# Feed-forward input products of a two-layer fp32 trunk: two row halves of TensorE, one accumulation bank each

## Chip, core and metric

The kernel runs on one core of a Trainium2 chip. The metric is the device time of one execution in microseconds (us), lower is better. The profile is of one execution on that core; its span runs from the first instruction to the last. All values are float32. The kernel multiplies them on TensorE in the fp32r format, as two parts.

## What is computed

A trunk of two layers over two streams of 256 tokens with 1024 channels: the context (which is computed by the same weights and is dropped at the end) and the latents (the output). Each layer is a half-step feed-forward, a token mixer, and a second half-step feed-forward; each is wrapped in a norm before, a norm behind, a shift, a scale and a gate. The feed-forward, on which the change bears:

```python
def sandwich(x, fn, mod3, g_pre, g_post, weight):
    shift, scale, gate = mod3
    h = rms_norm(x, g_pre) * (1 + scale) + shift
    return x + weight * gate * rms_norm(fn(h), g_post)

def swiglu(h, w_in, w_out):
    g, u = jnp.split(h @ w_in, 2, axis=-1)      # w_in 1024 x 5632
    return (jax.nn.silu(g) * u) @ w_out         # w_out 2816 x 1024
...
for l in range(DEPTH):                          # DEPTH = 2
    xl = sandwich(xl, ffn0, ...); xc = sandwich(xc, ffn0, ...)
    # the mixer: one input projection, recurrences and convolutions by groups of heads, one output projection
    xl = sandwich(xl, ffn1, ...)
    if not last:
        xc = sandwich(xc, ffn1, ...)
```

So there are four feed-forwards. The first three run on both streams (512 tokens), the last on the latents alone (256 tokens).

## The kernel before

**Layout.** Channels lie on the 128 partitions, tokens along the free axis: x, h and the outputs are 8 tiles of 128 channels by 512 tokens, the context's 256 and then the latents' 256. A weight tile of 128 x 128 is loaded into TensorE as the stationary operand and the 512 tokens stream past it.

**Precision by two parts.** Each operand is split in a high part that fp32r holds exactly and the rest (`split`, L169 to L174, ScalarE makes `hi` and VectorE `lo`). A product of two matrices is three passes: hi x hi, hi x lo, lo x hi. h has the parts `hh` and `hl`, weights `hi` and `lo`. A unit of weights is 1024 channels by 128 columns: with 8 tiles of channels and three passes it takes 24 products (`mm3`, L274), all added up in one bank of 512 float32 (`col_mm`, L282). `pbank` (L102) hands out banks of PSUM in turn; there are 6.

**A feed-forward** (`ffn`, L459) has 22 column pairs, a gate and an up unit each, in three parts of 6, 8 and 8 pairs (`PARTS`). For each pair the 44 units' weights come by DMA in `raw` tiles and are split; `col_mm` is called twice (L496); `evac` (L471 to L478) takes Silu of the gate's bank on ScalarE (L472), multiplies by the up bank on VectorE (L473) and splits the result into `ah`, `al`. At the end of each part the output phase (`out_phase`, L312) multiplies the part's 6 or 8 `ah`, `al` tiles by the output weights and adds them into the 8 tiles of `y`: by a ScalarE copy in the first part, by a VectorE addition (L325) in the others. The first 3 pairs of a feed-forward (6 units) go through `front` (L290) instead: their products are put in the order in which the tiles of the next h come.

**The pool `t`.** `tt_()` takes tiles of 128 x 512 float32 from one pool of `NT` = 28 buffers (L30). In a feed-forward it holds 8 tiles of `y`, the parts' `ah` and `al` (up to 16), and the sums of the norms (3). A tile that finds the pool full waits until the oldest tile's last reader is done. The mixers take their arrays from the same pool.

**The handover to the next sub-layer** (`Norms`, L351 to L442). While the last part's output tiles of y come, `add` (L378) makes three squares or products of a tile: two by ScalarE (L384, L386), one by VectorE (L387, `sq`, from a pool of 3 buffers), and adds them into three running sums `acc` (L390; two by GpSimd and one by VectorE, by `JACC`). The first tile's are written into the sums' tiles directly. Behind the last tile of a stream, `scales` (L394) sums over the partitions with products by ones (`st`), GpSimd takes the power -1/2 (`rsqrt`, L241), `update` (L418) broadcasts that over the partitions by TensorE (`rb`, L244 to L248) and begins the residual, and `forward` (L428) broadcasts the next input's scale and makes the tiles of the next h one by one (VectorE L270, L271, L262, L256). The two streams' last six output tiles are kept apart, so that the first stream's chain runs while TensorE does the second stream's products.

**What sets the order.** TensorE's instructions run in the order in which the code issues them. `Products` (L106) keeps a clock of the products issued (columns over 2400, in us), and `after` puts the steps of the norms (`LAG`, `STEP`) behind so much of later products. A wait in an instruction holds all that stands behind it on its engine. VectorE, ScalarE and GpSimd run their own queues in an order that the tile framework fixes when the program is built, from the order of the code and from when buffers come free.

Of the kernel before, what the change touches and what calls it, by code (L numbers as in the profile page):

```python
# [8 lines left out]
F32 = mybir.dt.float32  # L9
# [5 lines left out]
P = 128  # L15
# [14 lines left out]
NT, NRAW, NSPL = 28, 4, 6  # L30
SKEW = 6
# how much of the products (Products.clock) goes between the tiles of the next input, for the first stream and the second
STEP = (1.8, 0.4)
# places in h for tiles of the output
# [5 lines left out]
# how much of the products goes ahead of the sums over channels, of the first and of the second scales, likewise  # L40
# [3 lines left out]
# the last mixer's output tiles in banks  # L44
OUT_AT = ((0, 0), (0, 1), (1, 0), (1, 1), (2, 0), (3, 0), (4, 0), (5, 0))
# the last mixer's last tiles of the output, for all of its tiles in turn and then tile by tile
LATE = ((0,), (1, 2, 3))
MANUAL = {mybir.EngineType.PE}
# the parts of the mixers in the order in which they are issued: projections (small) and recurrences (capital)
# [3 lines left out]
# the last feed-forward's last units whose output products are put in the order of its tiles  # L53
TAIL = 4
# the last feed-forward's units behind which the residual is turned
TURN = 5
# tiles of modulation vectors made beside each feed-forward's units: in the first part, in the others, in the output phase
PUMP = {(0, 0): (2, 2, 2), (0, 1): (0, 2, 1), (1, 0): (0, 2, 1)}
# the start's steps, in the order in which they are issued: pairs of tiles of x (loads x, squares a), the tokens' scales (t, y),
# the conditioning vectors (c, rows d, e), units (loads u, parts w), the first modulation vectors for a pair of tiles by the  # L60
# tensor engine (loads q, products r, s, end f), their scale or shift for a tile by VectorE (loads v, b, sums V, B), pairs of
# tiles of h (h), the products that can be issued of the tiles before a given one (*), the mixer's small arrays (z) and decays (l)
# [5 lines left out]
# columns of the packed vectors, in units of [128, 1]  # L68
# [13 lines left out]
def backbone(ctx: ExitStack, tc: tile.TileContext, xT, vecs, crow, w_mod, w_in, w_out, w_mi, w_mo, w_lru, w_cm, b_cm, lam, w_last, out):  # L82
# [23 lines left out]
    class Products:  # L106
        """The tensor engine's queue, kept in the order of issue; what waits for other engines is put behind later products."""
# [4 lines left out]
        def matmul(self, dst, lhsT, rhs, start, stop):  # L112
            te.matmul(dst, lhsT=lhsT, rhs=rhs, start=start, stop=stop)  # L113
            self.clock += max(rhs.free_size(), 64) * (4 if rhs.dtype == F32 else 1) / 2400
            while not self.inside and self.later and self.later[0][0] <= self.clock:
                self.next()
# [59 lines left out]
    def load_split(src, shape, park=None):  # L176
        """A unit's two parts; park takes them to a place in h, idle at a phase's end: 0, 1 in the latents' half, 2, 3 in the other."""
        raw = wp.tile(shape, F32, tag="raw", name=nm("raw"), bufs=NRAW)
        nc.sync.dma_start(raw, src)
        if park is None:  # L180
            hi = wp.tile(shape, F32R, tag="hi", name=nm("hi"), bufs=NSPL)
            lo = wp.tile(shape, F32R, tag="lo", name=nm("lo"), bufs=NSPL)
        else:
            o = (P * park + SEQ) % T
            hi, lo = (t[:, :shape[1], o:o + P] for t in (hh, hl))
        h = shape[1] // 2
        for a, b in ((0, h), (h, shape[1])):
            split(raw[:, a:b], hi[:, a:b], lo[:, a:b])
        return hi, lo

# [53 lines left out]
    def broadcast(r):  # L244
        """[P tokens, 2] to [P, 256 tokens], on all partitions"""
        rb = ps_st.tile([P, SEQ], F32, tag="st", name=nm("rb"))
        for tt in range(2):
            te.transpose(rb[:, tt * P:(tt + 1) * P], r[:, tt:tt + 1].to_broadcast([P, P]), ident)  # L248
        return rb
# [24 lines left out]
    def mm3(dst, wh, wl, mh, ml, ks):  # L274
        """Three passes for two parts of each operand; the last of ks, which may come late, at the end."""
        ops = [(wh(k), x(k)) for k in ks[:-1] for x in (mh, ml)] + [(wl(k), mh(k)) for k in ks[:-1]]
        k = ks[-1]
        ops += [(wh(k), mh(k)), (wh(k), ml(k)), (wl(k), mh(k))]
        for i, (w, x_) in enumerate(ops):
            pe.matmul(dst, lhsT=w, rhs=x_, start=(i == 0), stop=(i == len(ops) - 1))  # L280

    def col_mm(w, a, b):  # L282
        """A loaded unit of 128 columns against the tokens a : b of h."""
        hi, lo = w
        p = pbank()
        mm3(p[:, :b - a], lambda k: hi[:, k, :], lambda k: lo[:, k, :],
            lambda k: hh[:, k, a:b], lambda k: hl[:, k, a:b], range(KT))
        return p

    def front(ws, plan, done):  # L290
        """The first units, channel by channel as h comes: plan has token ranges with units, done takes their products."""
        for a, b, us in plan:
# [9 lines left out]
            for k in range(KT):  # L302
                for i, (u, p) in enumerate(zip(us, aps)):
                    hi, lo = ws[u]
                    # one group a bank: its first product clears the bank
                    first, last = i % per == 0, i % per == per - 1 or i == len(us) - 1
                    for j, (w, h) in enumerate(((hi, hh), (hi, hl), (lo, hh))):
                        pe.matmul(p, lhsT=w[:, k, :], rhs=h[:, k, a:b],
                                  start=(first and k == 0 and j == 0), stop=(last and k == KT - 1 and j == 2))
            done(us, aps, a, b)  # L310

    def out_phase(ms, load, ah, al, y, nk, ranges_of, on_y, part, nparts, npump=0):  # L312
        """y[m] (+)= the product with the unit's weights, over token ranges; on_y(m, a, b) at the end."""
# [31 lines left out]
    # mean squares of the streams' tokens, with EPS  # L345
    msq = {}

    class Norms:
        """A sub-layer's output norm, residual and the next input norm, fed with the output tile by tile. With x' = x + r G y
        the mean square of x' is that of x, 2 r mean(x G y) and r^2 mean((G y)^2), so that both norms' scales come from sums  # L350
        over the tiles of y."""  # L351

        def __init__(self, segs, y, l, i, nxt, turn=False):
            self.segs, self.y, self.l, self.i, self.nxt = segs, y, l, i, nxt
            self.ready = False
            # whether a stream is the first or the second to come
# [87 lines left out]
    # the streams whose next input is on its way  # L444
# [4 lines left out]
    def unit_pieces(source):  # L449
        """Units for the next sub-layer, by halves."""  # L450
# [8 lines left out]
    def ffn(l, f, segs, nxt, plan, skew_out, turn=False):  # L459
# [5 lines left out]
        for part in range(NPART):  # L465
# [29 lines left out]
            for j in range(j0, nj):  # L495
                evac(j, *[col_mm(w, lo_t, hi_t) for w in load_in(j)], lo_t, hi_t)  # L496
# [12 lines left out]
    def ffn_last(l, f, plan):  # L509
        """The last feed-forward, on the latents, its output with the tokens on the partitions and gathered over all of the units  # L510
        in place, so that the output norm's scales need no way across the partitions."""
# [3 lines left out]
        # the residual, with the tokens on the partitions  # L515
# [64 lines left out]
        for tt in range(2):  # L580
            yg = [tt_() for _ in range(2)]
            for h in range(2):
                for j in range(max(NJ - TAIL, 0), NJ):
                    out_mm(j, tt, h)
                # 1 / 32 is the root of 1 / D
# [14 lines left out]
    def gain_row(l, v, s, h):  # L600
        """Half of a modulation vector as rows on all partitions."""
# [15 lines left out]
    def mixer(l, segs, nxt, plan, skew_out, order_of, next_unit=None):  # L617
        """segs: the streams whose output is wanted; both run the recurrence."""
# [24 lines left out]
        # the units of the input projection, then of the output projection, loaded two ahead of their use  # L643
# [66 lines left out]
        def lru_decay(c):  # L710
            for c, d, b in heads[2 * c:2 * c + 2]:
                e, r = tt_(), rs[c, d]
                # u = tanh(w / 2), e = exp(-w), w = 8 r softplus(-lambda); m = 1 - exp(-w) = u (1 + e)
# [3 lines left out]
                # (m - 2) m = -(1 - a^2)  # L717
# [87 lines left out]
        # the output projection of one stream: all tiles at once, the recurrent heads' part last, in float32's own  # L805
        # four passes
# [44 lines left out]
        # one stream: with x' = x + r G y the mean square of x' is that of x, 2 r mean(x G y) and r^2 mean((G y)^2),  # L851
        # so both norms' scales come from sums over the tiles of y
# [111 lines left out]
    def quarter_rows(q, k0):  # L964
        """Both vectors for two tiles by products with rows of weights, the inputs' chunks in turn on quarters of the columns."""
# [40 lines left out]
    def decays():  # L1006
        # softplus(-lambda) = max(-lambda, 0) + log1p(exp(-|lambda|)), log1p by its atanh series
# [157 lines left out]
def _layout(i):  # L1165
# [15 lines left out]
    # [l, vector, tile, output channel, inputs]; of the first two vectors some pairs of tiles by inputs: for each  # L1181
    # chunk of inputs [inputs, vector, tile, output channel], two such blocks a tile
# [14 lines left out]
    # [l, pair of heads, input, (direction, gate), output], block diagonal over the pair  # L1197
# [27 lines left out]
```

## Time and profile before

| | |
|---|---|
| median of 2 runs | 1649.24 us (1648.44 to 1650.04) |
| profiled execution, its span | 1648.9 us |
| TensorE busy | 1615.8 us, 98% |
| VectorE busy | 1165.1 us, 71% |
| ScalarE busy | 735.3 us, 45% |
| GpSimd busy | 121.2 us, 7% |
| read from memory | 247.39 MB, 151 GB/s over the span |

The profiled execution's own time is its span; what lies around it is within the 1.6 us by which the runs differ. Engines are PE (TensorE's products), PEld (TensorE's loads of weights, which can lie under products), DVE (VectorE), ACT (ScalarE), POOL (GpSimd) and SP (SyncE, which issues the DMAs). A busy PE is one with a product under way, which is more than the time that its stream of columns takes: products overlap, and the pitch from one start to the next is what they cost. An idle stretch of an engine is printed before the instruction that ended it, with what that instruction waited for. PEclk is the granted clock of TensorE as a share of full speed.

### The profile page before, as it was taken

Reading aid. Unit: us, or ns where it says so; the run is one execution under the profiler, and the core shown is the slowest. Engines: PE = TensorE matmul, PEld = TensorE weight load, DVE = VectorE, ACT = ScalarE, POOL = GpSimd, SP = SyncE. Lnnn points to the kernel's source line nnn. Section 1 sums busy time; section 2 is a strip of 40 time slices with the busy share of each in tenths; the row PEclk is TensorE's granted clock in tenths of the full one; section 3 lists DMA queues with packets and bytes.
Section 4 is the critical chain, followed back from the end, with each engine's and each line's share of the span. In section 5 each row is a group of like instructions: output and inputs, shape, how many; then the busy total and the mean of one; then the engine's idle time right before and its main releaser. Section 6 shows DMA issues by size and latency. Waiting matters only on the chain.

```text
span 1648.9 us, 23405 instructions
## 1 busy us (share of the span) xinstructions
PE 1615.8 (98%) x8832; PEld 1374.5 (83%) x8832; DVE 1165.1 (71%) x2183; ACT 735.3 (45%) x1377; POOL 121.2 (7%) x166
## 2 busy tenths in 40 slices
PE   6999999999999999999999999999999999999998
PEld 3788888889977998888888998888888998789997
DVE  4899898458689777867753887767433788875554
ACT  5524222244597662332233463322132469764543
POOL 0000000005000510000000410000000420000000
PEclk9999999999999999999999999999999999989999
DMA  9577666430323225655552215655422216245552
GB/s 369 187 226 264 201 228 219 146 127 28 103 71 110 86 88 191 209 168 175 182 163 80 99 46 198 219 167 176 140 90 90 103 52 202 80 138 195 179 192 77
DMA packets 73906, 249.97 MB, mean 152 GB/s; under 512 B 8384, under 2 KB 10048, under 8 KB 73792
## 3 DMA queue, kind: packets, MB, share of 16 engines
q1 hardware_dynamic: 73216, 247.94, 44.7%
q8 instruction: 69, 1.13, 0.3%
q10 hardware_dynamic: 576, 0.52, 0.1%
q14 instruction: 45, 0.37, 0.1%
HBM read 247.39 MB, written 1.05 MB: 151 GB/s over the span
## 4 chain that ended last, share of the span: by engine, by line
PE 90%; DVE 6%; ACT 2%; issue 1%; POOL 1%; DMA 0%; SPq 0%; POOLq 0%; DVEq 0%; ACTq 0%
PE mm L113 88%; PE st L113 1%; DVE x L271 1%; DVE sq L387 1%; DVE z L270 1%; DVE tmp L262 0%; DVE t L390 0%; DVE hl L256 0%; PE mod L113 0%; POOL rs L241 0%; DMA x<-in_xT 0%; ACT hh L263 0%; DVE ms L410 0%; DVE t L325 0%; POOL t L390 0%
## 5 line engine op out<-in xcount | busy, mean ns | idle before, releaser
L173 ACT CAST hi<-raw 128x512 fp32r<-128x512 f32 (+1 forms) x596 | 343.0, 610 | 675.0 <-PE mm L113 488.0
L113 PE MATMUL mm<-hh,hi 128*128 128x512 f32 (+1 forms) x1840 | 627.6, 350 | 1.1 <-ACT hh L263 1.1
L113 PE MATMUL mm<-hl,hi 128*128 128x512 f32 (+1 forms) x1840 | 626.0, 348 | 1.3 <-DVE hl L256 0.5
L174 DVE TENSOR_TENSOR lo<-raw,hi 128x512 fp32r<-128x512 f32 (+1 forms) x596 | 388.9, 683 | 158.3 <-ACT hi L173 155.2
L113 PE MATMUL mm<-hh,lo 128*128 128x512 f32 (+1 forms) x1840 | 469.3, 347 | 0.0
L113 PEld LDWEIGHTS mm<-hh,hi 128*128 128x128 f32 x1840 | 348.1, 190 | 52.5 <-ACT hh L1075 2.5
L113 PEld LDWEIGHTS mm<-hl,hi 128*128 128x128 f32 x1840 | 349.3, 190 | 50.9 <-DVE hl L1081 1.4
L113 PEld LDWEIGHTS mm<-hh,lo 128*128 128x128 f32 x1840 | 328.1, 190 | 47.2
L196 DVE SCALAR_TENSOR_TENSOR junk<-raw,cb 128x1024 bf16<-128x1024 f32 x256 | 312.8, 1222 | 69.0 <-DMA raw<-in_w_mod 65.4
L113 PE MATMUL mm<-t,hi 128*128 128x512 f32 (+1 forms) x1056 | 240.6, 367 | 0.0
L113 PEld LDWEIGHTS mm<-t,hi 128*128 128x128 f32 x1056 | 182.8, 188 | 35.7 <-issue 0.2
L390 POOL TENSOR_TENSOR t<-t,sq 128x256 f32<-128x256 f32 x112 | 95.0, 863 | 716.9 <-ACT sq L384 705.5
L113 PE MATMUL mm<-t,lo 128*128 128x512 f32 (+1 forms) x528 | 131.5, 367 | 0.0
L113 PEld LDWEIGHTS mm<-t,lo 128*128 128x128 f32 x528 | 92.6, 188 | 17.7
L473 DVE TENSOR_TENSOR sg<-sg,mm 128x512 f32<-128x512 f32 (+1 forms) x72 | 46.0, 639 | 82.9 <-PE mm L113 81.5
L113 PE MATMUL mm<-t,hh 128*128 128x256 f32 x512 | 72.1, 282 | 0.0
L113 PEld LDWEIGHTS mm<-t,hh 128*128 128x128 f32 x512 | 66.1, 188 | 0.5
L173 ACT CAST t<-sg 128x512 fp32r<-128x512 f32 (+1 forms) x94 | 50.7, 541 | 30.6 <-DVE sg L473 27.5
L263 ACT ACTIVATE hh<-tmp,modv 128x256 fp32r<-128x256 f32 x72 | 42.5, 597 | 34.6 <-DVE tmp L262 34.3
L325 DVE TENSOR_TENSOR t<-t,mm 128x256 f32<-128x256 f32 (+1 forms) x66 | 35.3, 536 | 29.2 <-PE mm L113 29.0
L174 DVE TENSOR_TENSOR t<-sg,t 128x512 fp32r<-128x512 f32 (+1 forms) x94 | 55.1, 587 | 1.0 <-ACT t L173 1.0
L113 PE MATMUL mm<-hi,t 128*128 128x512 f32 x176 | 55.1, 394 | 0.0
(177 smaller groups left out, 1199.3 us busy)
## 6 DMA issues: line engine op xcount, KB each, us to landing
raw<-in_w_in SPq DMA_DIRECT2D x176, 512.0 KB, 3.6
raw<-in_w_mod SPq DMA_DIRECT2D x128, 512.0 KB, 4.2
raw<-in_w_out SPq DMA_DIRECT2D x48, 512.0 KB, 3.3
raw<-in_w_mi SPq DMA_DIRECT2D x36, 512.0 KB, 4.2
raw<-in_w_last SPq DMA_DIRECT2D x22, 512.0 KB, 3.2
raw<-in_w_out SPq DMA_DIRECT2D x24, 384.0 KB, 3.6
t<-in_w_mod SPq DMA_DIRECT2D x32, 256.0 KB, 5.8
raw<-in_w_mo SPq DMA_DIRECT2D x8, 512.0 KB, 4.0
```

The lines of the kernel that those rows point to most:

```text
L113: te.matmul(dst, lhsT=lhsT, rhs=rhs, start=start, stop=stop)
L173: sc.copy(hi, src)
L174: ve.tensor_tensor(lo, src, hi.bitcast(F32), op=OP.subtract)
L196: ve.scalar_tensor_tensor(junk, raw.rearrange("p k c -> p (k c)"), 1.0, cb[:, s], op0=OP.mult, op1=OP.mult, accum_out=modv[l][:, v, m, s:s ...
L263: sc.activation(hh[:, m, a:b], tmp, AF.Identity, scale=A, bias=B)
L270: ve.tensor_tensor(z, y[m][:, a:b], rb, op=OP.mult)
L271: ve.scalar_tensor_tensor(x[:, m, a:b], z, mcol(l, 3 * i + 2, m, s), x[:, m, a:b], op0=OP.mult, op1=OP.add)
L325: ve.tensor_tensor(y[m][:, a:b], y[m][:, a:b], p[:, :b - a], op=OP.add)
L387: ve.scalar_tensor_tensor(q[2], y, G, x[:, m, a:b], op0=OP.mult, op1=OP.mult)
L390: (gp if JACC[c] == "g" else ve).tensor_tensor(acc[c], acc[c], q[c], op=OP.add)
L473: ve.tensor_tensor(sg[:, :b - a], sg[:, :b - a], pu[:, :b - a], op=OP.mult)
```

## The change

The units of the first three feed-forwards behind the staged first ones (`ffn`, L496 of before) go through a new function, `col_mm2`, with two banks. Each product on 128 rows (channels) becomes two, one on the rows 0 to 63 and one on the rows 64 to 127, with the same 512 columns; the first half's products are summed in one bank, the second half's in the other. The two follow one another, half by half, through all 24. Then ScalarE copies the first bank to a tile `half` in SBUF (from 2 buffers), VectorE adds the second bank to it, and `evac` reads those tiles where it read banks. The pool `t` has 26 buffers in place of 28. The clock of `Products` counts a product of 64 rows as half, so that the norms' steps fall behind as many units as before. `front`, the output phases, the mixers and the last feed-forward stay as they are. The remaining lines of the diff take comments away.

```diff
-NT, NRAW, NSPL = 28, 4, 6
+NT, NRAW, NSPL = 26, 4, 6
...
         def matmul(self, dst, lhsT, rhs, start, stop):
             te.matmul(dst, lhsT=lhsT, rhs=rhs, start=start, stop=stop)
-            self.clock += max(rhs.free_size(), 64) * (4 if rhs.dtype == F32 else 1) / 2400
+            self.clock += max(rhs.free_size(), 64) * (4 if rhs.dtype == F32 else 1) / 2400 * (0.5 if lhsT.shape[0] == 64 and lhsT.dtype == F32R else 1)
...
+    def col_mm2(w, a, b):
+
+        hi, lo = w
+        ps2 = [pbank(), pbank()]
+        for i, (t, h) in enumerate([e for k in range(KT) for e in ((hi[:, k], hh[:, k]), (hi[:, k], hl[:, k]))]
+                                   + [(lo[:, k], hh[:, k]) for k in range(KT)]):
+            for r, p in enumerate(ps2):
+                rows = slice(64 * r, 64 * r + 64)
+                pe.matmul(p[:, :b - a], lhsT=t[rows], rhs=h[rows, a:b], start=i == 0, stop=i == 3 * KT - 1)
+        t = hp.tile([P, T], F32, tag="half", name=nm("half"), bufs=2)
+        sc.copy(t[:, :b - a], ps2[0][:, :b - a])
+        ve.tensor_tensor(t[:, :b - a], t[:, :b - a], ps2[1][:, :b - a], op=OP.add)
+        return t
...
-                evac(j, *[col_mm(w, lo_t, hi_t) for w in load_in(j)], lo_t, hi_t)
+                evac(j, *[col_mm2(w, lo_t, hi_t) for w in load_in(j)], lo_t, hi_t)
```

How the order moves is shown at two places, with the names of the program and its numbers of buffers.

TensorE at the first changed unit of the first feed-forward, before (`mm` is a bank, `hh` and `hl` the parts of h, `hi` the weights):

```order
L113 MATMUL mm_458<-hh,lo_427 128x512
L113 MATMUL mm_626<-hh,hi_612 128x512
L113 MATMUL mm_626<-hl,hi_612 128x512
L113 MATMUL mm_626<-hh,hi_612 128x512
L113 MATMUL mm_626<-hl,hi_612 128x512
```

The same place after the change:

```order
L113 MATMUL mm_458<-hh,lo_427 128x512
L113 MATMUL mm_626<-hh,hi_612 128x512
L113 MATMUL mm_627<-hh,hi_612 128x512
L113 MATMUL mm_626<-hl,hi_612 128x512
L113 MATMUL mm_627<-hl,hi_612 128x512
```

Each product has become two, into the banks 626 and 627, in turn.

TensorE at the end of the first feed-forward, before (`st` are the products with ones of the first stream, from the three sums `t_2771` to `t_2773`; `mm_3082` is the bank of an output tile of the second stream):

```order
L113 MATMUL mm_3082<-t_2660,hl 128x256
L113 MATMUL mm_3082<-t_2733,hh 128x256
L113 MATMUL st_3105<-ones,t_2771 128x2 x2
L113 MATMUL st_3105<-ones,t_2772 128x2 x2
L113 MATMUL st_3105<-ones,t_2773 128x2 x2
L113 MATMUL mm_3082<-t_2734,hh 128x256
L113 MATMUL mm_3082<-t_2733,hl 128x256
L113 MATMUL mm_3138<-t_2170,hh 128x256
L113 MATMUL mm_3138<-t_2171,hh 128x256
```

The same step after the change (the sums are `t_3835` to `t_3837`, `mm_4394` is the bank of the second stream's last output tile, `rb` are the broadcasts, `hi_4451` and on the next sub-layer's weights):

```order
L113 MATMUL mm_4394<-t_3797,hh 128x256
L113 MATMUL mm_4394<-t_3798,hh 128x256
L113 MATMUL mm_4394<-t_3797,hl 128x256
L113 MATMUL st_4169<-ones,t_3835 128x2 x2
L113 MATMUL st_4169<-ones,t_3836 128x2 x2
L113 MATMUL st_4169<-ones,t_3837 128x2 x2
L248 MATMUL rb_4216<-ident,rs_4178 128x128 x2
L248 MATMUL rb_4251<-ident,rs_4188 128x128 x2
L113 MATMUL mm_4547<-hh,hi_4451 128x256
L113 MATMUL mm_4548<-hh,hi_4467 128x256
L113 MATMUL mm_4679<-hh,hi_4483 128x256
```

The products with ones and both broadcasts have moved from between the output tiles to behind the last of them, with the next input's products right after.

VectorE at the same place, before (`t_108` and `t_109` are tiles of y; L325 adds a bank to one; L387 writes a product for the third sum, `t_2773` itself for the first tile of each stream; `lo` are weights):

```order
L325 TENSOR_TENSOR t_108<-t_108,mm_2745 128x512
L174 TENSOR_TENSOR lo_3388<-raw_3385,hi_3387 128x512
L387 SCALAR_TENSOR_TENSOR t_2773<-t_108,modv_106,x 128x256 x2
L174 TENSOR_TENSOR lo_3388<-raw_3385,hi_3387 128x512
L174 TENSOR_TENSOR lo_3396<-raw_3393,hi_3395 128x512 x2
L174 TENSOR_TENSOR lo_3404<-raw_3401,hi_3403 128x512 x2
L325 TENSOR_TENSOR t_109<-t_109,mm_2788 128x512
```

And after the change, where L339 is the line of the bank's addition, L401 that of the product and L404 that of the sums:

```order
L339 TENSOR_TENSOR t_113<-t_113,mm_4300 128x256
L174 TENSOR_TENSOR lo_4492<-raw_4489,hi_4491 128x512 x2
L339 TENSOR_TENSOR t_114<-t_114,mm_4343 128x256
L401 SCALAR_TENSOR_TENSOR t_3837<-t_108,modv_106,x 128x256 x2
L401 SCALAR_TENSOR_TENSOR sq_3971<-t_111,modv_106,x 128x256
L404 TENSOR_TENSOR t_3836<-t_3836,sq_3970 128x256
L401 SCALAR_TENSOR_TENSOR sq_4014<-t_112,modv_106,x 128x256
L339 TENSOR_TENSOR t_115<-t_115,mm_4394 128x256
```

The third sum's first write stood behind the addition to the first tile of y (`t_108`); it now stands behind the addition to the last-but-one tile (`t_114`), just ahead of the last (`t_115`).

## Rows read from the trace of the kernel before

**Rows 1.** The page, part 1: busy us (share of the span) xinstructions.

```profile
PE 1615.8 (98%) x8832; PEld 1374.5 (83%) x8832; DVE 1165.1 (71%) x2183; ACT 735.3 (45%) x1377; POOL 121.2 (7%) x166
```

**Rows 2.** Timeline 133.5 to 134.2, PE and PEld: start us, us, engine line op.

```profile
133.55 0.40 PE L113 MATMUL mm<-hh,hi 128*128 128x512 f32 x1
133.56 0.19 PEld L113 LDWEIGHTS mm<-hl,hi 128*128 128x128 f32 x1
...
133.78 0.40 PE L113 MATMUL mm<-hl,hi 128*128 128x512 f32 x1
```

**Rows 3.** Windows: us, then PE, PEld, DVE, ACT, POOL, PEclk, DMA, GB/s.

```profile
82.00:164.00 82.00, 82.00 (x353) 66.06 (x353) 78.96 (x141) 26.53 (x50) 0.00 (x0) 1.00 0.74 243
164.00:247.00 83.00, 83.00 (x358) 66.86 (x357) 73.89 (x128) 24.04 (x43) 0.00 (x0) 1.00 0.65 214
```

**Rows 4.** The chain that ended last, 386 to 425: start us, us, what.

```profile
388.40 1.25 PE st L113 x12
...
413.12 6.30 PE mm L113 x29
...
419.64 3.42 PE mm L113 x29
```

**Rows 5.** Timeline of the same handover, PE, the broadcasts.

```profile
391.34 0.38 PE L248 MATMUL rb<-ident,rs 128*128 128x128 f32 x2
...
393.89 0.43 PE L248 MATMUL rb<-ident,rs 128*128 128x128 f32 x2 [0.41 <-POOL rs L241]
```

**Rows 6.** Groups by form, PE: busy us, mean ns | idle before.

```profile
L113 PE MATMUL mm<-hh,hi 128*128 128x512 f32 x1040 | 413.2, 397 | 0.0
...
L113 PE MATMUL mm<-t,wbd 128*128 128x512 f32 x64 | 28.5, 594 | 0.0
...
L113 PE MATMUL mod<-t,cs 128*32 128x512 f32 x64 | 9.7, 677 | 0.0
```

**Rows 7.** Timeline 34 to 37, PE: products on quarters of the columns.

```profile
34.03 1.92 PE L113 MATMUL mod<-t,cs 128*32 128x512 f32 x16
```

**Rows 8.** Groups by form, the other engines: busy us, mean ns | idle before.

```profile
L390 POOL TENSOR_TENSOR t<-t,sq 128x256 f32<-128x256 f32 x112 | 95.0, 863 | 716.9 <-ACT sq L384 705.5 <-DVE sq L387 9.4 <-DVE msq L413 2.0
...
L473 DVE TENSOR_TENSOR sg<-sg,mm 128x512 f32<-128x512 f32 x60 | 41.1, 684 | 81.6 <-PE mm L113 81.5
...
L387 DVE SCALAR_TENSOR_TENSOR sq<-t,modv,x 128x256 f32<-128x256 f32 x56 | 36.2, 646 | 4.1 <-ACT t L323 1.2 <-ACT sq L384 0.5
...
L271 DVE SCALAR_TENSOR_TENSOR x<-z,modv,x 128x256 f32<-128x256 f32 x64 | 33.8, 538 | 0.1
...
L256 DVE TENSOR_TENSOR hl<-tmp,hh 128x256 fp32r<-128x256 f32 x72 | 30.9, 433 | 6.8 <-ACT tmp L264 6.3
...
L262 DVE TENSOR_TENSOR tmp<-x,rb 128x256 f32<-128x256 f32 x72 | 29.3, 411 | 6.9 <-PE rb L248 6.8
...
L270 DVE TENSOR_TENSOR z<-t,rb 128x256 f32<-128x256 f32 x64 | 25.7, 411 | 4.5 <-PE rb L248 4.3
...
L323 ACT COPY t<-mm 128x512 f32<-128x512 f32 x26 | 15.1, 581 | 8.1 <-PE mm L113 8.1
```

**Rows 9.** Timeline 1445.5 to 1452, PE: the last mixer's handover.

```profile
1445.53 0.63 PE L605 MATMUL mm<-ident,modv 128*128 128x128 f32 x4
...
1449.21 0.69 PE L248 MATMUL rb<-ident,rs 128*128 128x128 f32 x2 [1.30 <-POOL rs L241]
1451.05 1.22 PE L113 MATMUL mm<-hh,hi 128*128 128x256 f32 x4 [1.15 <-ACT hh L263]
```

**Rows 10.** Windows, PE alone: us, PE busy (x), PEclk, DMA share, GB/s.

```profile
410.00:412.00 2.00, 1.27 (x11) 1.00 0.00 0
414.00:416.00 2.00, 2.00 (x11) 0.50 0.91 307
```

## The prediction

> **What bounds the kernel now.** I read the shares of the engines first. TensorE is busy for 98% of the span, VectorE for 71%, ScalarE for 45% [rows 1]. So a change is worth what it does to the stream of products, or what it puts into that stream as a wait. Second, what one product costs. In the units that the change rewrites a product of 512 columns starts 0.23 us after the one before it (133.55, 133.78) [rows 2], and the windows give the mean: 353 products in 82 us without a gap, 233 ns each [rows 3]. Each load of 128 x 128 weights lasts 0.19 us and begins within 0.01 us of the start of the product before the one that needs it, so it lies under that product [rows 2]. Third, where the slack is: VectorE has 3 us left of 82 in the first window and 9 of 83 in the second [rows 3]. Fourth, the handovers between sub-layers, where the output's last tiles, three running sums over the tiles, two scales and the next input follow one another. At 388.40 the 12 products with ones that finish a stream's sums take 1.25 us in the chain that ended last [rows 4], and the broadcasts follow at 391.34 and 393.89, among products [rows 5]. That overlap is what keeps TensorE at 98%.
>
> **The products.** 114 units change (three feed-forward layers of 44, less 6 each that stay in the first, staged part), each with 24 products: 2736 of the 3120 with 512 columns against h, whose first group of three has the row shown (x1040) [rows 6]. Each becomes two of 64 rows, so 2736 products and 2736 loads are added. The trace has no product of 64 rows. Its nearest rows are the products on quarters of the columns: 16 of them, whose mean duration is 677 ns, take 1.92 us together [rows 6, 7], and the 64 of that group are busy for 9.7 us, where 64 of the same kind on the whole array (the rows of t and wbd) are busy for 28.5 us [rows 6]. Parts of the array therefore run side by side at the price of one. From below, a pair costs the pure stream of 512 columns at 2.4 GHz, the level granted here [rows 3]: 213 ns, 20 less than now. From above, two in turn cost 466 ns. I take 234 to 235, nearest to the quarters: both halves stream the same 512 columns, and the two loads of a pair fit under it, since products of two columns, which only load, start every 104 ns (1.25 us for 12 [rows 4]), 208 for two. That is 2736 x 1.5 ns = **+4 us**, with ends of -55 and +637 us.
>
> The Trainium skill speaks for more (TensorE: Matmul & The Clock Gate, Part 3): weight loads overlap products in flight only where the row groups differ. By that rule loads would stand bare before the change and the halves would hide them. The trace disagrees: loads on all 128 rows lie under products on all 128 rows [rows 2], so I take no gain from it.
>
> **Taking the banks.** Each unit adds a copy of a bank by ScalarE, 581 ns like the copy of the output tiles, and an addition by VectorE, 684 ns like the product after Silu [rows 8]: 66 and 78 us over 114 units. ScalarE has the room. VectorE has not, in the first layer's windows: some 11 units end in the first, 7.5 us more against 3 us left, and 14 in the second, 9.6 us against 9 [rows 3]. A bank pair is wanted again two units later (6 banks, 2 a unit): 2 x 24 x 233 ns = 11.2 us of cover. The lag of some 5 us stays under it, but the addition stands behind weight halves and modulation sums in VectorE's queue. I take **+4 us**, between 0 and 15.
>
> **The smaller pool.** This is the largest term, and it is not in the products. NT falls from 28 to 26. At the end of a feed-forward 27 tiles of that pool are wanted: 8 of y, 16 of ah and al, 3 sums. With 26 the third sum gets its place only when al[0] is read for the last time, by the second of the 24 products of the last output tile. The order shows it: VectorE now writes the third sum after its addition of the last-but-one tile, and the products with ones stand behind the last output product with both broadcasts right behind them and the next input's products after those. Before, some 140 products of the second stream lay over this chain. All of it is now bare, at the ends of the first, second and third feed-forward. With E as the end of the last output product:
> - The third sum starts at E - 2.6 (22 products at 118 ns: 29 took 3.42 us [rows 4]). Two writes by VectorE, 0.65 us each [rows 8]; the first lets GpSimd begin at about E - 2.0.
> - GpSimd then has 13 additions before the first stream's sums are whole: 7 of the third sum, 5 of the first sum, held up because the 3 buffers for squares filled behind the third, and one of the second stream. At 95.0 us for 112 [rows 8], 0.85 each, that is 11.0 us: E + 9.0.
> - From the end of the sums to the first product of the next input the last mixer shows the bare chain: the products before it start at 1445.53 and last 0.63, the second broadcast waits 1.30 for GpSimd, the first product starts at 1451.05 [rows 9], about 5 us. Here half a microsecond of products with ones comes before, and two more GpSimd additions and about four VectorE operations (0.5 us each) of the second stream stand in it: 8 us. E + 17.
> - After an idle stretch the granted clock falls: TensorE is busy for 1.27 of the 2 us from 410, so idle for 0.73, the clock is 0.50 (the 1.2 GHz level) from 414 to 416, and 29 products take 6.30 us where the next 29 take 3.42 [rows 4, 10]. **+3 us**.
> - The second stream's sums lie behind the first's norm on VectorE (8 tiles of 0.41 + 0.54 + 0.41 + 0.43 = 1.79 us [rows 8] plus 5 us of sums, against 17 us of products): **+2 us**.
>
> That is 17 + 3 + 2 = 22 us, three times: **+66 us**, with ends of 10 and 32 each. At the end of the first mixer the sums run along as before, but the products with ones now stand inside the last tile of the second stream, with both broadcasts at its end: of the chain of 5 us some 1 us is covered, plus clock 3 and pace 3: **+10 us** (4 to 20). Inside the mixers the two missing tiles can make parts wait; the order of weights loaded differs there in one place only, so **+1 us** (0 to 10).
>
> Sum: 4 + 4 + 66 + 10 + 1 = +85 us on the profiled 1648.9, which is 0.3 below the median of the runs: **1734 us**.
>
> **The rivals.**
> - Halves in turn. Against it: the quarters of the columns [rows 6, 7]. For it: no row shows halves of the rows. 2736 x 233 = +637, plus 81 for the rest: 2367 us.
> - Halves side by side, but their loads bare, so that a pair costs 233 + 104 = 337 ns: +285 + 81, 2015 us. For it: the load path would be used for 208 of 233 ns, nearly without slack. Against it: loads under products on the same rows [rows 2]. The Trainium skill's page on TensorE (Part 3, measured speedup) gives 3.07-fold for four row tiles, so 1.30 of one product; an estimate from that page puts a pair between 1 and 1.30 of one, up to 303 ns, +192 us; no run here shows it.
> - Not slower: the pair runs at the bare stream of 213 ns because the 20 ns between products hide behind the other half. 2736 x -20 = -55, and the pool's +81 remains: 1675 us, within 2%. It decides from about 215 ns a pair. For it: 233 is 20 above 213. Against it: products of 256 columns start every 118 ns [rows 4], 11 above their 107, so the surplus goes with the columns, which halving the rows leaves as they are.
> - The pool does not bind as I say, because the sums are done soon after their place comes free: 5 us a handover in place of 22, 1649 + 4 + 4 + 25 = about 1682 us. Against it: GpSimd's 13 additions, which the order has behind the third sum.
>
> **How the numbers follow.** My forecast 0.74; halves in turn 0.08; loads bare or partly so 0.08; bare stream 0.06; pool not binding 0.04. About 2% is what a measurement here tells from no change, 33 us. The third and fourth of these lie at that edge, so within 2% gets 0.10, faster 0.02 (a pair would have to cost under 191 ns, below the stream itself), slower 0.88. The range reaches from 1685 (handovers at 12 us, or a pair at 217) to 1840 (handovers at 32, a pair at 260); the two dear cases above it hold most of the rest.
>
> **What would show it.** Right: in the second feed-forward windows of after a pair starts every 230 to 240 ns, the clock stays at 1.00, and TensorE's idle time, 33 us now, is over 80, nearly all in four handovers, before products with ones (released by GpSimd's additions) and before the next input's first products. The clock dips after each. Wrong: starts of a pair 213 or over 300 ns apart; no wait by products with ones for GpSimd; waits inside the units for VectorE's additions of over 15 us in all.

## The result, and the profile after

The changed kernel takes 1919.35 us (median of 2 runs, 1918.46 to 1920.23) against 1649.24 before: a ratio of 1.1639 (95% interval 1.1617 to 1.1661), 270 us slower. The forecast was 1734, range 1685 to 1840. The direction was right, the size was not.

The first part of the page of after, beside [rows 1]:

```profile
PE 1689.6 (88%) x11568; PEld 1416.5 (74%) x11568; DVE 1241.4 (65%) x2297; ACT 801.1 (42%) x1491; POOL 121.9 (6%) x166
```

TensorE has its 2736 products more (11568 in place of 8832) but is busy for only 74 us longer: the products as such did not double in price. It is idle for 227 us (1916.6 less 1689.6), where it was idle for 33. Where, the waits of PE say (engine line waited for: us in total, times, longest us):

```profile
PE mm L113 <- ACT t L173: 97.1, 12, 19.3
PE mm L113 <- DVE half L301: 50.6, 22, 6.7
PE st L113 <- POOL t L404: 27.3, 4, 9.0
PE st L113 <- DVE t L1057: 13.7, 1, 13.7
PE rb L248 <- POOL rs L241: 12.9, 10, 1.6
PE mm L113 <- ACT hh L263: 8.3, 5, 1.8
```

The third, fifth and sixth row are the handovers that the prediction spoke of; the fourth was there before (14.4 us). The first two make 148 us. The first, output products that wait for `ah`, the prediction did not have. The second, units that wait for a bank addition (`half`), is 50.6 us where it named over 15 as a sign of being wrong. The windows of [rows 3] show the same stretches of after (us, then PE, PEld, DVE, ACT, POOL, PEclk, DMA, GB/s):

```profile
82.00:164.00 82.00, 53.24 (x281) 41.08 (x278) 59.81 (x105) 18.29 (x38) 0.00 (x0) 0.81 0.55 170
164.00:247.00 83.00, 76.61 (x612) 60.09 (x610) 58.30 (x99) 25.33 (x48) 0.00 (x0) 1.00 0.50 159
```

TensorE loses 29 of the first 82 us. VectorE, which was expected to be full there, is busy for 60: it is late without being full. The timeline of PE has the longest of these waits, at the first output phase (start us, us, line, op):

```profile
120.29 0.40 PE L113 MATMUL mm<-t,hi 128*128 128x512 f32 x1
139.97 1.65 PE L113 MATMUL mm<-t,hi 128*128 128x512 f32 x3 [19.29 <-ACT t L173]
```

And the chain that ended last shows what held ScalarE's `t` (start us, us, what):

```profile
124.07 3.56 DMA raw<-in_w_mod
...
127.72 1.25 DVE junk L196 x2
...
131.53 1.24 DVE junk L196 x2
...
132.79 3.55 DMA raw<-in_w_mod
...
137.60 0.60 DVE half L301
...
138.66 0.61 DVE sg L487
...
139.30 0.63 ACT t L173
...
139.97 1.22 PE mm L113 x2
```

`junk` is VectorE's sum for a modulation vector (L196 in `mod_tile`): two for each 128 x 1024 tile, each after a DMA into the ring of 4 `raw` buffers that the weights share. The sums belong to the gate at this feed-forward's end and to later sub-layers; nothing at this place needs them. But they stand ahead of the addition in VectorE's queue, each tile's DMA starts when an earlier tile's sums have freed a buffer, and the addition, the multiplication (`sg`), ScalarE's `t` and TensorE wait behind the row of them.

The order of VectorE shows how they came there. Counted in it: the modulation sums that stand ahead of the multiplication of the fourth, fifth and sixth pair of the first feed-forward.

| | 4th | 5th | 6th |
|---|---|---|---|
| before | 6 | 13 | 20 |
| after | 13 | 24 | 33 |

Thirteen more sums at 1.22 us with their DMAs have to be done before the sixth pair's `ah`, for which the output products wait. At the other parts' ends the shift is smaller: 8 sums in the second part of the first feed-forward, 3 or 4 in the first two parts of the next two, none in the third parts. A few are enough. At the end of the second feed-forward's first part it is 4, and TensorE waits for 13.9 us at 786.26, since the DMAs stand one behind another there too (the chain that ended last):

```profile
768.69 3.82 DMA raw<-in_w_mod
...
776.63 4.19 DMA raw<-in_w_mod
```

What the prediction feared most did not come. The timeline of PE and PEld in after, a stretch without waits (a row x2 is one pair, which the units' order puts side by side):

```profile
80.53 0.40 PE L113 MATMUL mm<-hh,hi 64*128 64x512 f32 x2
80.54 0.19 PEld L113 LDWEIGHTS mm<-hl,hi 64*128 64x128 f32 x2
80.77 0.40 PE L113 MATMUL mm<-hl,hi 64*128 64x512 f32 x2
```

A pair starts every 0.23 us, as a product did [rows 2], and both loads begin within 0.01 us of it. The gain is zero and so is the price: at the full clock pairs in after and products before both start every 233.3 ns in the mean.

### The profile page after: what moved, and what is told of

Read it like the earlier page. It is cut to its first block, busy times and chain, and to the rows that moved or that the text cites. A ratio compares the mean times of both kernels' runs of the same rounds, so it can differ in the third digit from the quotient of the medians.

```text
span 1916.6 us, 29041 instructions
## 1 busy us (share of the span) xinstructions
PE 1689.6 (88%) x11568; PEld 1416.5 (74%) x11568; DVE 1241.4 (65%) x2297; ACT 801.1 (42%) x1491; POOL 121.9 (6%) x166
## 4 chain that ended last, share of the span: by engine, by line
PE 55%; DVE 17%; DMA 17%; issue 5%; ACT 3%; POOL 2%; DVEq 0%; SPq 0%; POOLq 0%; ACTq 0%
PE mm L113 53%; DMA raw<-in_w_mod 16%; DVE junk L196 8%; DVE lo L174 3%; DVE half L301 2%; POOL t L404 1%; ACT hi L173 1%; PE st L113 1%; ACT sg L486 1%; PE mod L113 1%; DVE hl L174 1%; DMA raw<-in_w_in 0%; DVE sg L487 0%; DVE sq L401 0%; DVE t L174 0%
## 5 line engine op out<-in xcount | busy, mean ns | idle before, releaser
L113 PE MATMUL mm<-hh,hi 64*128 64x512 f32 (+2 forms) x2752 | 696.9, 375 | 59.1 <-DVE half L301 50.6
L113 PE MATMUL mm<-hl,hi 64*128 64x512 f32 (+2 forms) x2752 | 694.4, 372 | 1.6 <-DVE hl L256 1.0
L113 PEld LDWEIGHTS mm<-hh,hi 64*128 64x128 f32 (+1 forms) x2752 | 449.7, 194 | 126.6 <-DVE half L301 61.7
L113 PEld LDWEIGHTS mm<-hl,hi 64*128 64x128 f32 (+1 forms) x2752 | 452.3, 193 | 51.4 <-DVE hl L256 3.4
L113 PE MATMUL mm<-hh,lo 64*128 64x512 f32 (+2 forms) x2752 | 464.8, 362 | 0.0
L196 DVE SCALAR_TENSOR_TENSOR junk<-raw,cb 128x1024 bf16<-128x1024 f32 x256 | 313.3, 1224 | 228.8 <-DMA raw<-in_w_mod 224.8
L113 PEld LDWEIGHTS mm<-hh,lo 64*128 64x128 f32 (+1 forms) x2752 | 343.0, 188 | 45.6
L113 PE MATMUL mm<-t,hi 128*128 128x512 f32 (+1 forms) x1056 | 257.8, 383 | 102.2 <-ACT t L173 97.1
L404 POOL TENSOR_TENSOR t<-t,sq 128x256 f32<-128x256 f32 x112 | 94.5, 864 | 1374.2 <-ACT sq L398 1316.2
L486 ACT ACTIVATE sg<-half 128x512 f32<-128x512 f32 x57 | 36.1, 633 | 196.2 <-DVE half L301 196.2
L339 DVE TENSOR_TENSOR t<-t,mm 128x256 f32<-128x256 f32 (+1 forms) x66 | 35.6, 540 | 82.8 <-PE mm L113 82.7
L301 DVE TENSOR_TENSOR half<-half,mm 128x512 f32<-128x512 f32 x114 | 77.6, 681 | 11.3 <-ACT half L300 11.3
L300 ACT COPY half<-mm 128x512 f32<-128x512 f32 x114 | 66.2, 581 | 29.0 <-PE mm L113 29.0
```

The costliest lines, as they stand in the source:

```text
L196: ve.scalar_tensor_tensor(junk, raw.rearrange("p k c -> p (k c)"), 1.0, cb[:, s], op0=OP.mult, op1=OP.mult, accum_out=modv[l][:, v, m, s:s ...
L300: sc.copy(t[:, :b - a], ps2[0][:, :b - a])
L301: ve.tensor_tensor(t[:, :b - a], t[:, :b - a], ps2[1][:, :b - a], op=OP.add)
L339: ve.tensor_tensor(y[m][:, a:b], y[m][:, a:b], p[:, :b - a], op=OP.add)
L404: (gp if JACC[c] == "g" else ve).tensor_tensor(acc[c], acc[c], q[c], op=OP.add)
L486: sc.activation(sg[:, :b - a], pg[:, :b - a], AF.Silu)
```

## Experiments

All times are medians (e7 and e8: of one run each, so without an interval) beside runs of the kernel before on the same chip, which gave 1648.7 to 1651.0. Theory A is that the order of VectorE's and ScalarE's queues costs what is not the small pool; its rivals are the additions and the pairs themselves.

**e1, the small pool alone.**

```diff
 (before)
-NT, NRAW, NSPL = 28, 4, 6
+NT, NRAW, NSPL = 26, 4, 6
```

> The kernel before with the pool of 26 buffers and nothing else. Its order has the products with ones and both broadcasts of the first stream behind the last output product at the ends of the first three feed-forwards, as after the change. Theory (the pool is worth what the prediction said, 22 us a handover): 1649 + 66 + 10 + 1 = about 1726 us. Rival (the chain is shorter, as the waits by products with ones in the changed kernel, 27.3 us over 4, and the broadcasts' 12.9 suggest: some 12 to 15 us a handover with the clock): 1685 to 1700 us.

Measured: 1707.65 us, ratio 1.0356 (1.0340 to 1.0371), +59. Between the two expectations. The timeline of PE at the first handover:

```profile
402.14 0.28 PE L113 MATMUL mm<-t,hl 128*128 128x256 f32 x1
411.35 2.72 PE L113 MATMUL st<-ones,t 128*128 128x2 f32 x12 [8.93 <-POOL t L390]
415.35 0.69 PE L248 MATMUL rb<-ident,rs 128*128 128x128 f32 x2 [1.28 <-POOL rs L241]
417.65 0.69 PE L248 MATMUL rb<-ident,rs 128*128 128x128 f32 x2 [1.61 <-POOL rs L241]
420.14 1.01 PE L113 MATMUL mm<-hh,hi 128*128 128x256 f32 x3 [1.81 <-ACT hh L263]
```

From the end of the last output product (402.42) it is 8.93 us to the end of GpSimd's sums, and 17.7 to the next input's first product: the 9.0 and 17 of the prediction. (Its terms behind the sums, 5, 0.5, 1.7 and 2 us, make 9 and not the 8 that it took; 8.8 were measured.) The net is smaller. By the starts of equal-numbered products in the two traces the three handovers cost 14, 16 and 17 us, not 22 each, the first mixer's end 8 in place of 10, and the second mixer's, which the prediction did not count, 3. About 2 of the 17 us are products with ones and broadcasts that TensorE had to run before as well (1.25, 0.38 and 0.43 us) [rows 4, 5]. The low clock was there before at the first handover [rows 10] and, for 3.4 us from 958.5, at the second, so its 3 us were in part counted twice; at the third (1334 to 1338) the clock before was 1.00. No run shows the 2 us for the second stream.

**e2, no copy and no addition** (the sums over the channels 64 to 127 of each tile are left out).

```diff
 (col_mm2 of after)
-        t = hp.tile([P, T], F32, tag="half", name=nm("half"), bufs=2)
-        sc.copy(t[:, :b - a], ps2[0][:, :b - a])
-        ve.tensor_tensor(t[:, :b - a], t[:, :b - a], ps2[1][:, :b - a], op=OP.add)
-        return t
+        return ps2[0]
```

> The changed kernel without the copy and the addition: the second bank is left out of the result, so the sums over half of the channels are missing. Theory A (the order: on VectorE's queue more of the modulation sums stand ahead of each pair's multiplication than before, 13, 24 and 33 in the first part in place of 6, 13 and 20, and TensorE comes to the output phase before VectorE has made ah): the stalls stay, 1850 to 1920 us. Theory B (the additions themselves hold the banks and VectorE): only the small pool is left, 1690 to 1735 us.

Measured: 1927.50 us, ratio 1.1683 (1.1650 to 1.1716), 8 us above theory A's range and far from theory B's. Without a single addition the kernel is no faster. The waits of PE have the same two at the head, the multiplication now in the addition's place:

```profile
PE mm L113 <- ACT t L173: 107.4, 12, 17.0
PE mm L113 <- DVE sg L484: 57.6, 14, 11.9
```

So it is not the additions' work. In its order the sums stand at 13, 24 and 32.

**e3, products on all 128 rows, two banks, added.**

```diff
-            for r, p in enumerate(ps2):
-                rows = slice(64 * r, 64 * r + 64)
-                pe.matmul(p[:, :b - a], lhsT=t[rows], rhs=h[rows, a:b], start=i == 0, stop=i == 3 * KT - 1)
+            r, n = divmod(i, 3 * KT // 2)
+            pe.matmul(ps2[r][:, :b - a], lhsT=t, rhs=h[:, a:b], start=n == 0, stop=n == 3 * KT // 2 - 1)
```

> The changed kernel with its 24 products on all 128 rows, twelve in each bank, the banks added as in the change, the pool of 26. The modulation sums ahead of each multiplication are 7, 12 and 19 in the first part, as before the change. Theory A (the order): e1 and up to 20 us more for the additions, 1690 to 1745 us. Theory B (the additions): near the changed kernel, 1870 to 1930 us. If the pairs themselves were what costs, also 1690 to 1745, but then the next run stays slow.

Measured: 1709.91 us, ratio 1.0370 (1.0355 to 1.0386), 2 us above e1, which is within the spread of the runs. All 114 copies and additions are there and cost some 2 us or nothing. The order has the sums at 7, 12 and 19.

**e4, the sums held.** The edge puts an instruction behind another on the same engine in the order of issue and makes no wait.

```diff
 (mod_tile of after; SIDE, the list of the counts before the change, is in `held` with the multiplications)
...
+            for mult in [mu for lim, mu in held if lim <= sums[0]][-1:]:
+                tc.add_manual_dep(ins.ins, mult.ins.name, mybir.DependencyInfo(mybir.DependencyClass.NoSync,
+                                  mybir.DependencyReason.DATA), reason="side")
+            sums[0] += 1
...
```

> The changed kernel with an edge of order on VectorE alone: each modulation sum stays on the side of the unit pairs' multiplications on which it stood before the change (6, 13, 20, 46 and so on); pairs, additions and the pool of 26 stay. Theory A (the order): the waits for ah and for the additions go, 1690 to 1745 us. Theory B (additions) or slow pairs: no change, 1880 to 1930 us.

Measured: 1775.85 us, ratio 1.0774 (1.0758 to 1.0790). Of the 209 us between the change and e3's level, 143 are gone with nothing changed but the places of the sums. 66 remain, and the time is 31 us above the range of theory A. The timeline of PE at the first output phase:

```profile
115.57 0.79 PE L113 MATMUL mm<-t,hi 128*128 128x512 f32 x1 [10.99 <-ACT t L173]
```

**e5 and e6, weight halves held too, pools of 26 and 27.** As e4, with the same edge from each weight half (ScalarE's `hi`, VectorE's `lo`) to the pairs' Silu and multiplication, by the counts of before; e6 has `NT` = 27.

> As e4, and the weight halves by ScalarE and VectorE are kept on their sides of each pair's Silu and multiplication as well (24, 28, 32 and so on, where the change has 26, 30, 34); pairs, additions and the pool of 26 stay. In e4 the one wait left at the first output phase, 10.99 us, followed ScalarE's halves of output weights that had to come by DMA. Theory A (the order of both): 1705 to 1725 us, like e3 with its products on all rows. Rival (the pairs cost something that the order does not hold, a pitch of over 233 ns or the loads): stays at 1750 to 1780 us.

> As e5 with 27 buffers in the pool, so that the third sum finds a place when the first output tile comes. Pairs and additions stay. Theory A: nothing is left but pairs and additions, 1649 to 1660 us. Rival (pairs at the bare stream of 213 ns, a gain covered so far by the waits): 1595 to 1630 us. Rival (the additions fill VectorE): 1665 to 1690 us.

Measured: 1805.55 us, ratio 1.0953 (1.0938 to 1.0968), and 1744.90 us, ratio 1.0587 (1.0570 to 1.0605). Both miss theory A's ranges, and e5 is 30 us worse than e4. The timeline of VectorE in e6 shows what these edges leave free:

```profile
83.41 0.69 DVE L506 TENSOR_TENSOR sg<-sg,half 128x512 f32<-128x512 f32 x1
84.02 1.22 DVE L213 SCALAR_TENSOR_TENSOR junk<-raw,cb 128x1024 bf16<-128x1024 f32 x1
...
94.07 0.68 DVE L320 TENSOR_TENSOR half<-half,mm 128x512 f32<-128x512 f32 x1
```

The counts hold between multiplications, as before, but now there are two additions between two multiplications, and all seven sums stand ahead of the first of them. ScalarE's Silu waits for that addition. The sums stand so in e4 as well, so this can explain why e4 too stays above e3, but not the 30 us. What e5 adds is that weight halves stand behind that Silu, and TensorE's wait for `half` is longer; e4 and then e5:

```profile
PE mm L113 <- DVE half L309: 5.0, 4, 2.8
```

```profile
PE mm L113 <- DVE half L320: 19.7, 8, 5.4
```

That the held weight halves make these 15 us is likely and was not tried apart; the other 15 are open. Holding half of an order is not holding the order. The pool's 61 us (e5 less e6) are free of this.

**e7, the weight halves held and the sums left early.**

> As e5, but with the weight halves alone on their sides; the modulation sums stand as early as the change puts them (14, 24, 32 ahead of the first part's multiplications). Theory A: the early sums are the larger part, so most of the loss stays, 1840 to 1920 us. If the weight halves are the cause: 1705 to 1760 us.

Measured: 1937.25 us (one run), 17 us above theory A's range and far from the other. Holding the weight halves alone wins nothing; the early sums are the larger part.

**e8, the halves one behind the other.** As e6, with the loop over the halves outside the loop over the 24 products.

> As e6, but each unit's 24 products on the rows 0 to 63 come first and the 24 on the rows 64 to 127 behind them, so that neighbours in the queue lie on the same half. If two products run side by side only when they lie on different halves: 2736 x 233 ns more, 2270 to 2300 us, with starts 233 ns apart. If a product on 64 rows of itself takes half the time: 1649 to 1670 us.

Measured: 2112.54 us (one run), below the first expectation and far above the second; the last section has its rows.

**e9 and e10, e3's order for the pairs, pools of 27 and 26.** Weight halves and sums have edges to each copy, addition, Silu and multiplication, with the counts taken from e3's order (`PLACES`):

```diff
...
+            for kind in ("add", "mult"):
+                behind(ins, kind, PLACES[kind][1], sums[0])
+            sums[0] += 1
...
```

> Pairs and additions as in the change, the pool of 27. Weight halves and modulation sums are kept on their sides not only of Silu and multiplication (as e5 and e6), but of each copy and addition too, with the places that they have in e3; e6 had seven sums ahead of the gate's addition where e3 has two, two and three between the additions. Theory A (the order is all that is left): 1649 to 1660 us. Rival (pairs drive VectorE or the loads in some other way): stays at 1700 to 1745 us.

> As e9 with the pool of 26. Theory A: like e3, 1705 to 1720 us, so that e3's products on all rows and pairs cost the same. Rival: 1760 to 1805 us.

Measured: e9 1669.19 us, ratio 1.0120 (1.0102 to 1.0138); e10 1727.48 us, ratio 1.0478 (1.0457 to 1.0500). The same pairs, banks and additions as the change, and 192 us less (1919.4 to 1727.5) by the places in two queues alone. Theory A holds for that, but both runs lie above its ranges, by 9 and 7 us: some 18 us are left that it had not (1727.5 against e3's 1709.9; 1669.2 against e11's 1650.7). The waits of PE in e9 name 10.5 of them, which e11 does not have:

```profile
PE mm L113 <- ACT t L195: 6.7, 6, 2.7
...
PE mm L113 <- DVE t L196: 3.8, 6, 1.2
```

They are again output products at the start of a phase, so a rest of the order that the edges do not hold (the casts of `ah` were not held) is likely; it was not tried. Behind the waits near 234, 784 and 1167 us the clock is 0.50 or 0.51 for 3.4 us each, which is part of the rest. The time that VectorE's sums wait for their DMAs is 65.4 us before, 224.8 in after and 46.6 in e10; the last two groups, after first:

```profile
L196 DVE SCALAR_TENSOR_TENSOR junk<-raw,cb 128x1024 bf16<-128x1024 f32 x256 | 313.3, 1224 | 228.8 <-DMA raw<-in_w_mod 224.8
```

```profile
L218 DVE SCALAR_TENSOR_TENSOR junk<-raw,cb 128x1024 bf16<-128x1024 f32 x256 | 312.9, 1222 | 49.2 <-DMA raw<-in_w_mod 46.6
```

**e11, e3 with the pool of 27.**

> e3 with the pool of 27: products on all rows, twelve in each of two banks, added. If the additions cost nothing where the order is right: 1647 to 1655 us. If they cost what the prediction said: 1653 us. If e3's closeness to e1 hid a loss behind the handovers: 1660 to 1680 us.

Measured: 1650.73 us against 1650.97, ratio 1.0001 (0.9989 to 1.0013). With a place for the third sum and the order right, two banks and 114 additions cost nothing that shows.

**e12, the change with the pool of 27.**

> The changed kernel with the pool of 27 and nothing else. If pool and order add up: 1919 - 60 = 1860 us, within 12. If the waits for VectorE swallow those of the handovers: 1880 to 1920 us.

Measured: 1855.35 us, ratio 1.1237 (1.1214 to 1.1260). The pool is worth 64 us here, 58 between e10 and e9, 59 in e1: pool and order add up.

## Why the prediction was right or wrong

| step | predicted | measured |
|---|---|---|
| pairs at 234 to 235 ns | +4 | 233 ns a pair, no cost of its own; +18 between e3 and e10, cause in part open (e9 against e11: 10.5 in waits for `ah`) |
| copies and additions | +4, 0 to 15 | +2 or nothing (e1 to e3), 0 (e11) |
| smaller pool, handovers and mixers | +77 | +59 (e1) |
| places in VectorE's and ScalarE's queues | not a term | +192 (e10 to the change) |
| sum | +85 | 270 |

The steps are a chain of kernels from before to after, so that they add up, to 271 by the rounded terms, is no test of them.

- **The products.** Right: the halves run side by side, a pair at the pitch of a product, loads under it. The Trainium skill (TensorE: Matmul & The Clock Gate, Part 3: Packing small matmuls, the mechanism) has in one line that loads overlap a product only where the row groups differ; the paragraph ahead of it also lets a load go ahead into the background weight buffer. The trace does not agree with the line: the loads for all 128 rows lay under products on all 128 rows before (0.01 us behind their start) [rows 2], and the halves' loads do so after. So there was nothing to gain, and taking no gain from that rule was right.
- **The pool.** Right in place and mechanism, the stretch at the handover almost to the microsecond (17.7 for 17). The net is 59 for 77, too large by work of TensorE and a low clock that were in part there before, and by a delay of the second stream that no run shows.
- **The additions.** The work was sized right. The step that failed is the sentence behind it: that the addition stands behind weight halves and modulation sums in VectorE's queue and that this costs 4 us, at most 15. It took VectorE's queue as before with 114 additions put in. The queue was another, and its places cost 192 us; without any addition (e2) the time is no shorter. The order of after was at hand, and the prediction read it at the handovers but not at the ends of the parts, where 13, 24 and 33 sums in place of 6, 13 and 20 stood to be counted.
- **The clock.** It came as a follower: with 227 us of idle time the mean granted clock is 0.934, with 33 us before 0.992. In after it is 0.52 from 98 to 100 us, behind a wait of 3.06 us that ended at 93.79, and pairs start 0.43 us apart there. Between the profiled executions of e10 and after TensorE's idle time grows by 141 us and its busy time, with the same products, by 52 (1637.8 to 1689.6). So about a quarter of what the places cost is not waiting but slower products behind the waits.
- **The range.** Its lower end, 1685, is given for handovers at 12 us or a pair at 217 ns. The pair gives it; handovers at 12 us give 1704.

Why the framework reordered can be told from orders alone. Twice as many instructions are not enough: a kernel with all 128 rows and two products of 256 columns for each of 512 (its order was read from the program as built; it was not run) has the sums at 7, 13 and 20. Twice the products at all 512 columns (after, e2) have 13, 24 and 32 or 33. The framework seems to reckon each half product at the full price of its columns, so that by its reckoning a unit takes twice as long and VectorE has room for later sums ahead of the unit's end. The chip runs the two at once, TensorE arrives in half that time, and finds VectorE still at the sums. That the reckoning as such is the cause is inferred from the orders; that the order is the cost is shown by e4, e9 and e10.

The rival that ended on the other side, pairs at 213 ns, did not come: the pitch in after and e9's 1669 us both speak against it.

## What to carry to other kernels

Where a framework orders the queues by its own reckoning, a change on one engine can reorder another that the diff does not touch: count, in the new order, what stands ahead of each instruction that the busiest engine waits for, at every phase's end and not only where a term is expected. An engine with idle time can still be the one that is late, if what stands first in its queue waits for a transfer. And one buffer less in a shared pool can move a whole chain off its cover: 26 in place of 27 cost 58 to 64 us here (e9 and e10, e5 and e6, e12), 27 in place of 28 nothing that shows (e11).

## What the runs showed of the hardware

Two products of 64 rows on different halves start about 3 ns apart (the median in e9, 1 to 12) and together cost what one of 128 rows costs, 0.23 us at the full clock; the pair wins nothing. When the queue holds 24 products of one half and then 24 of the other (e8), TensorE does not run them strictly in turn. The timeline of PE at such a border, where `hh,lo` is the end of one half's products and `hh,hi`, `hl,hi` the beginning of the other's:

```profile
81.17 0.49 PE L113 MATMUL mm<-hh,hi 64*128 64x512 f32 x1
81.39 0.39 PE L113 MATMUL mm<-hh,lo 64*128 64x512 f32 x1
81.50 0.39 PE L113 MATMUL mm<-hl,hi 64*128 64x512 f32 x1
81.63 0.39 PE L113 MATMUL mm<-hh,lo 64*128 64x512 f32 x1
81.74 0.39 PE L113 MATMUL mm<-hh,hi 64*128 64x512 f32 x1
81.86 0.39 PE L113 MATMUL mm<-hh,lo 64*128 64x512 f32 x1
81.97 0.39 PE L113 MATMUL mm<-hl,hi 64*128 64x512 f32 x1
...
85.94 0.49 PE L113 MATMUL mm<-hh,hi 64*128 64x512 f32 x1
```

The second half's first products start while three of the first half's, which stand ahead of them in the queue, have not started. So 24 products take 4.77 us from border to border (81.17 to 85.94) in place of 24 x 0.233 = 5.6, and the kernel 2112.5 us (one run) in place of the 2270 to 2300 expected. The Trainium skill (TensorE: Matmul & The Clock Gate, Part 3: Packing small matmuls, the mechanism) states that products start and end strictly in their order; by these starts that does not hold across halves, and the measurement decides.
